# Forgetting attention: the causal mask moves from a matrix product into the own block's key terms

## The chip, the cores and the metric

One core of one Trainium2 chip. The metric is the device time of one launch in microseconds, the median of the runs shown.

## What is computed

The kernel computes two transformer blocks on 1024 tokens of width 1024 in float32. The first has 16 meta tokens in front, a Mamba-2 branch and a softmax attention with forget gates; the second has a differential and a dilated attention. The change touches the forgetting attention alone: 16 heads of 64, 1040 positions, taken in blocks of 128 queries.

```python
c = jnp.cumsum(logf, axis=1)
...
s = jnp.einsum("bthd,bshd->bhts", qi, k).astype(jnp.float32) * scale
s = s + (cqi[..., :, None] - c_k[..., None, :])
s = jnp.where(kpos[None, :] <= qpos[:, None], s, -jnp.inf)
p = jax.nn.softmax(s, axis=-1).astype(v.dtype)
return jnp.einsum("bhts,bshd->bthd", p, v)
```

The query's own term `cqi` is the same for all keys of a row and falls out of the softmax; the key term `-c_k` stays.

## The kernel before, in words

The heads are taken in eight pairs `p`, two heads `j` at a time. Each pair goes through the projections of its keys, queries and values (`fox_project`), the gate (`fox_gate`) and the attention (`fox_attend`). Generators yield after each step, and `merge` weaves the attention of a pair with the gate projection of the same pair (two halves, each 24 products of 512 columns, lines 112 to 114), then with the projections of the next pair. The engines run in the order in which this weaving writes the instructions; nothing is rescheduled later.

In `fox_attend` the key terms of a head are loaded into `cb`, the same row on all 128 partitions. A pair has eight query tiles `i`, each in three steps. `A(i)` makes the negated logits of 16 + 128(i+1) keys: for each head the keys are cut into one to three chunks of at most 512 columns, each in a PSUM bank of its own; two products (lines 566 and 567, the high and low parts of the operands) fill it, and for the last chunk a third product of a bf16 identity with a bf16 table adds 1e30 to the 128 columns of the query's own block where the key comes after the query (line 569). VectorE then adds the key terms to the bank, writes the sum to `N` and takes the running minimum of the row (line 570). Each reduction is followed by an instruction that reads the accumulator into one column of `mn`, and the reduction of the next chunk takes that column as its scalar. ScalarE computes the exponentials with the last column as bias (line 573), and GpSimd copies the 16 meta columns (line 576). `B(i)` transposes the blocks of `N` on TensorE (line 624) and evacuates them on ScalarE into `pt` (line 630). `C(i)` multiplies with the values for every fourth tile (lines 604 and 607), and VectorE multiplies the result with the gate (line 609).

`pipeline` writes these steps as A(0), A(1), then for each i: A(i+2), C(i-1), B(i). For one pair the order on TensorE is: A(0), first half of the gate, A(1), A(2), B(0), A(3), second half of the gate, B(1), A(4), B(2), A(5), B(3), A(6), C(3), B(4), A(7), B(5), then the projections of the next pair. The gate's halves are evacuated by ScalarE (line 519), then by VectorE (line 520).

The PSUM pool has eight banks in this part (line 75), all of one tag; each call of `bank` takes the next of the eight in turn, and the first writer waits until the last reader of that bank's previous content is done.

```python
self.psum(8, 0)
...
b = self.ps.tile([128, 512], F32, tag="bank", name="bank", bufs=self.one)
```

GpSimd's queue holds the 16-column copies and the subtractions that split the weights into a high and a low part (line 121); SyncE issues the loads of the weights and of `cb`.

Of the kernel before, what the change touches and what calls it, by code (L numbers as in the profile page):

```python
# [9 lines left out]
F32 = mybir.dt.float32  # L10
F32R = mybir.dt.float32r
BF16 = mybir.dt.bfloat16
I32 = mybir.dt.int32
AF = mybir.ActivationFunctionType
ALU = mybir.AluOpType
# [10 lines left out]
HUGE = 3e38  # L26
# [40 lines left out]
class Kern:  # L67
# [128 lines left out]
    def consts(self):  # L196
        nc, V, cst = self.nc, self.nc.vector, self.cst
        self.w32 = cst.tile([128, 32], F32, name="w32")
        V.memset(self.w32, 0.0)
        V.memset(self.w32[0:64, 0:1], 1.0)  # L200
        V.memset(self.w32[64:128, 1:2], 1.0)
        V.memset(self.w32[:, 2:3], 1.0)
        self.identb = cst.tile([128, 128], BF16, name="identb")
        self.maskb = cst.tile([128, 128], BF16, name="maskb")
        V.tensor_copy(out=self.identb, in_=self.ident)
        V.tensor_copy(out=self.maskb, in_=self.cm[:, 3, :])
        self.ones = cst.tile([128, 128], F32, name="ones")
        V.memset(self.ones, 1.0)
        a, b = PARAM_COLS["conv_w"]
        self.cwh = cst.tile([128, 120], F32, name="cwh")  # L210
        V.tensor_scalar(out=self.cwh, in0=self.params[:, a:a + 120], scalar1=0.5, scalar2=None, op0=ALU.mult)
        self.gbh = cst.tile([128, 16], F32, name="gbh")
        V.tensor_scalar(out=self.gbh, in0=self.pslot("gate_bias"), scalar1=0.5, scalar2=None, op0=ALU.mult)
        self.sb48 = cst.tile([48, 1], F32, name="sb48")
        V.tensor_tensor(out=self.sb48, in0=self.pslot("b48")[:48], in1=self.pslot("sgn")[:48], op=ALU.mult)
# [322 lines left out]
    def fox_attend(self, p, st):  # L538
        nc, te = self.nc, self.nc.tensor
        cb = []  # L540
        for j in range(2):
            c = self.ph.tile([128, L], F32, tag="cb", name="cb", bufs=2)
            nc.sync.dma_start(out=c, in_=self.d_csp[2 * p + j].partition_broadcast(128))
            cb.append(c)
        vT = st.pop("vT")
        st["vm"] = self.v_meta(vT)
        st["v"] = self.v_tokens(vT, [16 + 128 * b for b in range(8)])
        y = self.slot("y", w=T)
        Ns, PTs, M = {}, {}, [None, None]

        def A(i):
            if i % 4 == 0:
                M[i // 4] = self.ph.tile([128, 2, 128], F32, tag="bt", name="pm", bufs=2)
            W = 16 + 128 * (i + 1)
            n = -(-W // 512)
            w = -(-W // (2 * n)) * 2
            Ns[i] = []
            for j in range(2):
                N = self.slot("N")
                mn = self.sm.tile([128, 3], F32, tag="mn", name="mn", bufs=4)  # L560
                qt = st["q"][j][:, i * 128:(i + 1) * 128]
                for c in range(n):
                    s0, s1 = c * w, min(W, c * w + w)
                    S = self.bank()[:, :s1 - s0]
                    last = c == n - 1
                    te.matmul(S, qt, st["k"][j][0][:, s0:s1], start=True, stop=False)
                    te.matmul(S, qt, st["k"][j][1][:, s0:s1], start=False, stop=not last)
                    if last:
                        te.matmul(S[:, s1 - s0 - 128:], self.identb, self.maskb, start=False, stop=True)
                    nc.vector.tensor_tensor_reduce(  # L570
                        out=N[:, s0:s1], in0=cb[j][:, s0:s1], in1=S, scale=1.0,
                        scalar=mn[:, c - 1:c] if c else HUGE, op0=ALU.add, op1=ALU.min, accum_out=mn[:, c:c + 1])
                nc.scalar.activation(out=N[:, :W], in_=N[:, :W], func=AF.Exp, scale=-1.0, bias=mn[:, n - 1:n],  # L573
                                     accum_out=self.lall[:, 2 * p + j, i:i + 1])
                c = 32 * (i % 4) + 16 * j
                nc.gpsimd.tensor_copy(out=M[i // 4][:, 0, c:c + 16], in_=N[:, 0:16])
                Ns[i].append(N)
            return 4 * max(W, 512) / 2.4

        def B(i):  # L580
            if i % 4 == 3:
                ps = self.bank()
                te.transpose(ps[:, :128], M[i // 4][:, 0], self.ident)
                nc.vector.tensor_copy(out=M[i // 4][:, 1], in_=ps[:, :128])
            if i % 4 == 0:

                PTs[i // 4] = [[self.ph.tile([128, 4, 512], F32, tag="pt", name="pt", bufs=4) for _ in range(2)]
                               for _ in range(i // 4 + 1)]
            q = slice((i % 4) * 128, (i % 4 + 1) * 128)
            for j in range(2):  # L590
                self.transposes(Ns[i][j], 16, i + 1, [pt[j][:, :, q] for pt in PTs[i // 4]], act=True)
            del Ns[i]
            return 2 * (i + 1) * 109

        def C(i):
            if i % 4 != 3:
                return 0
            g = i // 4
            pt = PTs.pop(g)
            O = self.bank()  # L600
            for b in range(i + 1):
                c0 = max(0, b - 4 * g) * 128
                for j in range(2):
                    te.matmul(O[64 * j:64 * j + 64, c0:], st["v"][:, b, 64 * j:64 * j + 64],
                              pt[b // 4][j][:, b % 4, c0:], start=b == 0, stop=False)
            for t in range(4):
                te.matmul(O[:, t * 128:(t + 1) * 128], st["vm"][:, t], M[g][:, 1], start=False, stop=t == 3)
            c = slice((i - 3) * 128, (i + 1) * 128)
            nc.vector.scalar_tensor_tensor(out=y[:, c], in0=O, scalar=0.5, in1=st["zs"][:, c], op0=ALU.mult,
                                           op1=ALU.mult)  # L610
            return (2.5 + 4 * g) * 910

        yield from self.pipeline(8, A, B, C)
        nc.sync.dma_start(out=self.d_yatt[p], in_=y)

# [1198 lines left out]
```

## Time and profile before

| | us |
|---|---|
| median of 3 runs (2728.5 to 2733.69) | 2733.47 |
| the profiled execution | 2729.51 |
| its span | 2727.7 |

| engine | busy us | share of the span |
|---|---|---|
| TensorE, products | 2659.8 | 98% |
| VectorE | 1372.3 | 50% |
| ScalarE | 1165.6 | 43% |
| GpSimd | 684.5 | 25% |

PE is TensorE, PEld its weight loads, DVE VectorE, ACT ScalarE, POOL GpSimd. Products are pipelined: the next one starts before the one ahead has ended, and a product's end is modelled, so the time that it costs is read from the starts that follow each other. The forgetting attention lies between some 75 and 655 us of the span, in eight pairs of about 77 us. The granted clock of TensorE is full (0.994 over the execution).

### The profile page before, as it was taken

The numbers are of one execution on the slowest core, as the hardware profiler recorded it, in microseconds if no ns is written. First come the engines' busy times: TensorE is split into PE (matmuls) and PEld (weight loads), VectorE is DVE, ScalarE is ACT, GpSimd is POOL, SyncE is SP. The second block draws the span as 40 slices with busy tenths as digits, with TensorE's granted clock in tenths as the row PEclk, the third lists the DMA queues.
The fourth block names the chain that finished last, engine by engine and source line by source line (L and its number), as shares of the span: only waits on it lengthen the run. The fifth ranks groups of instructions, "written<-read, shape, count | busy, mean of one in ns | idle before, by whom it ended". The sixth has DMA issues, their size and how long they took to land. (4 is left out here: it accounts for less than half of the span.)

```text
span 2727.7 us, 38674 instructions
## 1 busy us (share of the span) xinstructions
PE 2659.8 (98%) x14925; PEld 2232.2 (82%) x14925; DVE 1372.3 (50%) x2761; ACT 1165.6 (43%) x2080; POOL 684.5 (25%) x764
## 2 busy tenths in 40 slices
PE   8999999999999999999999999999999999998999
PEld 6888888888989889889877887878877877777877
DVE  5433322233574573654756777444654555446332
ACT  5554444445343433443432123445644555445331
POOL 1112121111243342342432333111111121204321
PEclk9999999999999999999999999999999999998999
DMA  3122222221123123122168653340222223324422
GB/s 131 58 64 72 78 79 71 78 64 62 39 88 114 55 78 116 55 103 91 55 207 279 205 182 131 128 121 30 72 70 70 79 94 94 86 72 146 160 65 70
DMA packets 85464, 266.87 MB, mean 98 GB/s; under 512 B 10880, under 2 KB 12032, under 8 KB 84256
## 3 DMA queue, kind: packets, MB, share of 16 engines
q1 hardware_dynamic: 85280, 264.40, 30.3%
q8 instruction: 117, 1.92, 0.3%
q14 instruction: 67, 0.55, 0.1%
HBM read 205.57 MB, written 33.49 MB: 88 GB/s over the span
## 5 line engine op out<-in xcount | busy, mean ns | idle before, releaser
L121 POOL TENSOR_TENSOR wlo<-wraw,whi 128x1024 fp32r<-128x1024 f32 (+2 forms) x168 | 374.4, 2232 | 1288.7 <-ACT whi L120 1077.8
L112 PE MATMUL bank<-uh,whi 128*128 128x512 f32 (+4 forms) x1752 | 625.8, 357 | 0.1
L114 PE MATMUL bank<-uh,wlo 128*128 128x512 f32 (+4 forms) x1752 | 618.8, 353 | 0.1
L113 PE MATMUL bank<-ul,whi 128*128 128x512 f32 (+4 forms) x1752 | 618.5, 353 | 0.0
L114 PEld LDWEIGHTS bank<-uh,wlo 128*128 128x128 f32 (+1 forms) x1752 | 327.9, 187 | 35.4 <-POOL wlo L121 0.5
L112 PEld LDWEIGHTS bank<-uh,whi 128*128 128x128 f32 (+1 forms) x1752 | 328.3, 187 | 34.3 <-issue 1.1
L113 PEld LDWEIGHTS bank<-ul,whi 128*128 128x128 f32 (+1 forms) x1752 | 328.2, 187 | 32.3
L112 PE MATMUL bank<-u,whi 128*128 128x512 f32 x512 | 207.8, 406 | 0.7 <-ACT pr L935 0.7
L113 PE MATMUL bank<-u,whi 128*128 128x512 f32 x512 | 203.6, 398 | 0.0
L114 PE MATMUL bank<-u,wlo 128*128 128x512 f32 x512 | 203.3, 397 | 0.0
L120 ACT ACTIVATE whi<-wraw 128x1024 fp32r<-128x1024 f32 (+2 forms) x169 | 155.3, 926 | 20.5 <-DMA wraw<-in_w_pa_dram 18.2
L630 ACT ACTIVATE pt<-bank 128x512 f32<-128x512 f32 (+1 forms) x320 | 143.0, 509 | 44.8 <-PE bank L624 38.1
L114 PE MATMUL bank<-yh,wlo 128*128 128x512 f32 x384 | 152.5, 397 | 1.0 <-POOL wlo L121 0.8
L112 PE MATMUL bank<-yh,whi 128*128 128x512 f32 x384 | 152.3, 397 | 0.9 <-ACT whi L120 0.9
L113 PE MATMUL bank<-yl,whi 128*128 128x512 f32 x384 | 151.9, 395 | 0.0
L647 DVE SCALAR_TENSOR_TENSOR acc<-raw,cwh,acc 128x1040 f32<-128x1040 f32 x72 | 93.7, 1302 | 109.5 <-ACT acc L644 107.8
L573 ACT ACTIVATE N<-N,mn 128x272 f32<-128x272 f32 (+7 forms) x128 | 100.3, 786 | 45.2 <-DVE mn L570 44.0
L114 PEld LDWEIGHTS bank<-u,wlo 128*128 128x128 f32 x512 | 97.2, 190 | 23.2
L112 PEld LDWEIGHTS bank<-u,whi 128*128 128x128 f32 x512 | 97.8, 191 | 22.3 <-ACT pr L935 1.1
L113 PEld LDWEIGHTS bank<-u,whi 128*128 128x128 f32 x512 | 97.6, 191 | 20.7
L121 POOL TENSOR_TENSOR wo<-wl,wo 128x512 fp32r<-128x512 f32 x52 | 73.4, 1425 | 157.8 <-ACT wo L120 150.6
L624 PE MATMUL bank<-cm,N 128*128 128x128 f32 x832 | 106.9, 273 | 0.0
(326 smaller groups left out, 4961.5 us busy)
## 6 DMA issues: line engine op xcount, KB each, us to landing
wraw<-in_w_in_dram SPq DMA_DIRECT2D x120, 512.0 KB, 4.1
gt<-d_gate SPq DMA_DIRECT2D x48, 512.0 KB, 5.7
ab<-d_acs SPq DMA_DIRECT2D x32, 512.0 KB, 3.5
qs<-qt SPq DMA_DIRECT2D x48, 256.0 KB, 2.9
wl<-in_w_out_dram SPq DMA_DIRECT2D x48, 256.0 KB, 5.4
tab<-in_tab_dram SPq DMA_DIRECT2D x8, 1056.0 KB, 5.9
cb<-d_csp SPq DMA_DIRECT2D x16, 520.0 KB, 7.6
d_gate<-gt SPq DMA_DIRECT2D x16, 512.0 KB, 2.9
```

Source lines behind the costliest of these rows:

```text
L112: te.matmul(ps, lh, rh, start=start, stop=False)
L113: te.matmul(ps, lh, rl, start=False, stop=False)
L114: te.matmul(ps, ll, rh, start=False, stop=stop)
L120: self.nc.scalar.activation(out=hi, in_=src, func=AF.Copy)
L121: (self.nc.vector if vector else self.nc.gpsimd).tensor_tensor(out=lo, in0=src, in1=hi.bitcast(F32), op=ALU.subtract)
L573: nc.scalar.activation(out=N[:, :W], in_=N[:, :W], func=AF.Exp, scale=-1.0, bias=mn[:, n - 1:n], accum_out=self.lall[:, 2 * p + j, i:i + 1])
L624: nc.tensor.transpose(ps[:, b * 128:(b + 1) * 128], N[:, c:c + 128], self.ident)
L630: self.nc.scalar.activation(out=out, in_=ps, func=AF.Copy)
L647: V.scalar_tensor_tensor(out=acc[:, :L], in0=raw[:, k:k + L], scalar=w(k), in1=acc[:, :L], op0=ALU.mult, op1=ALU.add)
```

## The change

The identity and the mask in bf16 and the third product go away. For each query tile and head GpSimd adds the mask table to the 128 key terms of the own block, into a tile `cd` (`own_terms`). `A(i)` writes the sums of tile i+1 ahead of its own work, and `A(0)` those of tiles 0 and 1. VectorE's reduction of the last chunk is cut in two, the keys ahead of the own block with `cb` as before and the own block's 128 keys with `cd`; the running minimum goes through both, so `mn` has a fourth column.

```diff
-        self.identb = cst.tile([128, 128], BF16, name="identb")
-        self.maskb = cst.tile([128, 128], BF16, name="maskb")
-        V.tensor_copy(out=self.identb, in_=self.ident)
-        V.tensor_copy(out=self.maskb, in_=self.cm[:, 3, :])
...
+        CD = {}
+
+        def own_terms(i):
+
+            CD[i] = [self.sm.tile([128, 128], F32, tag="cd", name="cd", bufs=4) for _ in range(2)]
+            for c, k in zip(CD[i], cb):
+                nc.gpsimd.tensor_tensor(out=c, in0=k[:, 16 + 128 * i:144 + 128 * i], in1=self.cm[:, 3], op=ALU.add)
+
         def A(i):
...
+            if i == 0:
+                own_terms(0)
+            if i < 7:
+                own_terms(i + 1)
+            cds = CD.pop(i)
...
-                    last = c == n - 1
                     te.matmul(S, qt, st["k"][j][0][:, s0:s1], start=True, stop=False)
-                    te.matmul(S, qt, st["k"][j][1][:, s0:s1], start=False, stop=not last)
-                    if last:
-                        te.matmul(S[:, s1 - s0 - 128:], self.identb, self.maskb, start=False, stop=True)
-                    nc.vector.tensor_tensor_reduce(
-                        out=N[:, s0:s1], in0=cb[j][:, s0:s1], in1=S, scale=1.0,
-                        scalar=mn[:, c - 1:c] if c else HUGE, op0=ALU.add, op1=ALU.min, accum_out=mn[:, c:c + 1])
-                nc.scalar.activation(out=N[:, :W], in_=N[:, :W], func=AF.Exp, scale=-1.0, bias=mn[:, n - 1:n],
+                    te.matmul(S, qt, st["k"][j][1][:, s0:s1], start=False, stop=True)
+                    ends = [(s0, s1, cb[j][:, s0:s1])] if c < n - 1 else [(s0, s1 - 128, cb[j][:, s0:s1 - 128]),
+                                                                          (s1 - 128, s1, cds[j])]
+                    for a, b, k in ends:
+                        if a == b:
+                            continue
+                        nc.vector.tensor_tensor_reduce(
+                            out=N[:, a:b], in0=k, in1=S[:, a - s0:b - s0], scale=1.0,
+                            scalar=mn[:, m - 1:m] if m else HUGE, op0=ALU.add, op1=ALU.min, accum_out=mn[:, m:m + 1])
+                        m += 1
+                nc.scalar.activation(out=N[:, :W], in_=N[:, :W], func=AF.Exp, scale=-1.0, bias=mn[:, m - 1:m],
```

Three places of the instruction order show it, all from the first pair of heads; in brackets stand the queues that an instruction waits for. The first is VectorE at the first head of tiles 2 and 3 (line 582 is the reduction after the change; the short rows read the accumulator). Before:

```order
L570 ISA N_885,mn<-cb,bank 128x400 [waits DVE_49,PE_49]
L570 ISA mn 128x1
...
L570 ISA N_911,mn<-cb,bank 128x264 [waits PE_49,Activation_49]
L570 ISA mn 128x1
L570 ISA N_911,mn<-cb,bank,mn 128x264 [waits DVE_49,PE_49]
L570 ISA mn 128x1
```

Now:

```order
L582 ISA N_897,mn<-cb,bank 128x272 [waits PE_49]
L582 ISA mn 128x1
L582 ISA N_897,mn<-cd,bank,mn 128x128 [waits DVE_49,Pool_49]
L582 ISA mn 128x1
...
L582 ISA N_927,mn<-cb,bank 128x264 [waits PE_49,Activation_49]
L582 ISA mn 128x1
L582 ISA N_927,mn<-cb,bank,mn 128x136 [waits DVE_49,PE_49]
L582 ISA mn 128x1
L582 ISA N_927,mn<-cd,bank,mn 128x128 [waits DVE_49,Pool_49]
L582 ISA mn 128x1
```

Each head of each tile has one reduction and one read more, and the added piece waits for the read ahead of it and for GpSimd.

The second is TensorE after the change, from tile 3 to the second half of the gate projection (lines 575 and 576 were 566 and 567).

```order
L575 MATMUL bank<-kx_261,qs_559 128x264 [waits PE_49]
L576 MATMUL bank<-ky_262,qs_559 128x264
L575 MATMUL bank<-kx_261,qs_559 128x264 [waits DVE_49]
L576 MATMUL bank<-ky_262,qs_559 128x264
L575 MATMUL bank<-kx_263,qs_561 128x264 [waits DVE_49,PE_49]
L576 MATMUL bank<-ky_264,qs_561 128x264
L575 MATMUL bank<-kx_263,qs_561 128x264 [waits DVE_49,PE_49]
L576 MATMUL bank<-ky_264,qs_561 128x264
L112 MATMUL bank<-uh_1_88,whi_649 128x512 [waits DVE_49,PE_49]
```

The two masks that stood behind every last chunk are gone; the order is otherwise as before, and the projection's first product waits for VectorE.

The third is GpSimd. Before, the copies of tiles 0 to 2:

```order
L576 COPY pm<-N_811 128x16 [waits Activation_49,Pool_49]
L576 COPY pm<-N_820 128x16 [waits Activation_49]
L121 TENSOR_TENSOR wlo_831<-wraw_657,whi_830 128x1024 [waits DMAHW7_49,Activation_49]
L576 COPY pm<-N_867 128x16 [waits Activation_49]
L576 COPY pm<-N_876 128x16 [waits Activation_49]
L576 COPY pm<-N_885 128x16 [waits Activation_49]
```

Now:

```order
L553 TENSOR_TENSOR cd<-cb,cm 128x128 x2
L589 COPY pm<-N_815 128x16 [waits Activation_49]
L589 COPY pm<-N_824 128x16 [waits Activation_49]
L121 TENSOR_TENSOR wlo_835<-wraw_653,whi_834 128x1024 [waits DMAHW7_49,Activation_49]
L553 TENSOR_TENSOR cd<-cb,cm 128x128 [waits Pool_49]
L553 TENSOR_TENSOR cd<-cb,cm 128x128 [waits DVE_49]
L589 COPY pm<-N_875 128x16 [waits Activation_49]
L589 COPY pm<-N_884 128x16 [waits Activation_49]
L553 TENSOR_TENSOR cd<-cb,cm 128x128 [waits Pool_49]
L553 TENSOR_TENSOR cd<-cb,cm 128x128 [waits DVE_49]
L589 COPY pm<-N_897 128x16 [waits Activation_49]
```

The sums of tile i+1 stand between the copies of tile i-1 and those of tile i.

## Rows read from the trace of the kernel before

**Rows 1.** Page, part 1: busy us, share of the span, instructions of each engine.

```profile
PE 2659.8 (98%) x14925; PEld 2232.2 (82%) x14925; DVE 1372.3 (50%) x2761; ACT 1165.6 (43%) x2080; POOL 684.5 (25%) x764
```

**Rows 2.** Waits of PE, 70 to 655 us: us in total, times, longest.

```profile
PE bank L604 <- ACT pt L630: 5.6, 8, 0.8
PE bank L566 <- DVE mn L570: 1.4, 1, 1.4
```

**Rows 3.** Timeline of PE, first stretch: start us, us, line, tiles, [idle before].

```profile
317.57 0.28 PE L566 MATMUL bank<-kx,qs 128*128 128x264 f32 x1
317.69 0.28 PE L567 MATMUL bank<-ky,qs 128*128 128x264 f32 x1
317.81 0.23 PE L569 MATMUL bank<-maskb,identb 128*128 128x128 bf16 x1
317.85 0.37 PE L566 MATMUL bank<-kx,qs 128*128 128x264 f32 x1
318.06 0.28 PE L567 MATMUL bank<-ky,qs 128*128 128x264 f32 x1
...
318.42 0.23 PE L569 MATMUL bank<-maskb,identb 128*128 128x128 bf16 x1
318.46 0.48 PE L112 MATMUL bank<-uh,whi 128*128 128x512 f32 x1
318.78 0.39 PE L113 MATMUL bank<-ul,whi 128*128 128x512 f32 x1
319.01 0.39 PE L114 MATMUL bank<-uh,wlo 128*128 128x512 f32 x1
```

**Rows 4.** Timeline of DVE, first stretch (tile 1 from 316.91).

```profile
316.91 0.43 DVE L570 CUSTOM_DVE_ANT_0 N<-cb,bank 128x272 f32<-128x272 f32 x1
...
318.12 0.08 DVE L570 DVE_READ_ACCUMULATOR2_ANT mn<- 128x1 f32 x1
...
318.61 0.42 DVE L570 CUSTOM_DVE_ANT_0 N<-cb,bank 128x264 f32<-128x264 f32 x1
318.96 0.08 DVE L570 DVE_READ_ACCUMULATOR2_ANT mn<- 128x1 f32 x1
319.19 0.49 DVE L570 CUSTOM_DVE_ANT_0 N<-cb,bank,mn 128x264 f32<-128x264 f32 x1
319.60 0.08 DVE L570 DVE_READ_ACCUMULATOR2_ANT mn<- 128x1 f32 x1
```

**Rows 5.** Groups by form, DVE, 70 to 655 us: busy us, mean ns, idle before.

```profile
L570 DVE CUSTOM_DVE_ANT_0 N<-cb,bank,mn 128x456 f32<-128x456 f32 x16 | 11.0, 689 | 2.7 <-DVE mn L570 0.5
L570 DVE CUSTOM_DVE_ANT_0 N<-cb,bank,mn 128x264 f32<-128x264 f32 x16 | 7.8, 489 | 2.3
```

**Rows 6.** Timeline of DVE, second stretch and behind it.

```profile
324.92 0.69 DVE L520 SCALAR_TENSOR_TENSOR zs<-zs,bank 128x512 f32<-128x512 f32 x1 [4.25 <-ACT zs L519]
...
330.29 0.08 DVE L570 DVE_READ_ACCUMULATOR2_ANT mn<- 128x1 f32 x1
...
336.09 0.69 DVE L609 SCALAR_TENSOR_TENSOR y<-bank,zs 128x512 f32<-128x512 f32 x1 [2.73 <-PE bank L607]
```

**Rows 7.** Timeline of PE, second stretch.

```profile
323.86 0.40 PE L114 MATMUL bank<-uh,wlo 128*128 128x512 f32 x1
...
332.04 2.85 PE L604 MATMUL bank<-pt,vtok 128*64 128x512 f32 x16 [0.75 <-ACT pt L630]
```

**Rows 8.** Timeline of ACT, second stretch.

```profile
330.47 0.94 ACT L573 ACTIVATE N<-N,mn 128x784 f32<-128x784 f32 x1
...
331.40 1.07 ACT L630 ACTIVATE pt<-bank 128x512 f32<-128x512 f32 x2
```

**Rows 9.** Groups by form, POOL, whole span: busy us, mean ns, idle before.

```profile
L761 POOL TENSOR_TENSOR yq<-yq,th 128x128 f32<-128x128 f32 x128 | 60.7, 508 | 124.1 <-DVE yq L758 124.1
```

**Rows 10.** Timeline of POOL: the last copy of tile 3.

```profile
321.66 0.20 POOL L576 COPY pm<-N 128x16 f32<-128x16 f32 x1 [0.63 <-ACT N L573]
```

More of the change, by code (lines that the diff above doesn't have):

```diff
@@ L559, in A @@
                 N = self.slot("N")
-                mn = self.sm.tile([128, 3], F32, tag="mn", name="mn", bufs=4)
+                mn = self.sm.tile([128, 4], F32, tag="mn", name="mn", bufs=4)
                 qt = st["q"][j][:, i * 128:(i + 1) * 128]
+                m = 0
                 for c in range(n):
```

## The prediction

> **What bounds the kernel now.** I read the busy totals of the page first, then PE's waits in the attention part, then three timelines of one head pair, engine by engine. The totals [rows 1] say PE 98%, DVE 50%, POOL 25%: over the whole run TensorE is the limit. The waits of PE between 70 and 655 us [rows 2] say the same of this part: 5.6 us in eight waits for `pt`, 1.4 us in one wait for `mn`, nothing else. A reader who stops here concludes that 128 products fewer on PE are simply time won. The eight waits are the warning. There is one in each head pair, always at the product with the values (line 604), and it ends with ACT, not with PE. The eight pairs repeat a pattern of some 77 us, so I work one of them out, the one from 309 us on, and multiply.
>
> **What a mask product costs PE** [rows 3]. Inside a chunk of 264 keys the second product starts 0.12 us after the first (317.57, 317.69). The mask starts at 317.81, the next product at 317.85, and its follower at 318.06, 0.21 later instead of 0.12. So the mask takes 0.04 us itself and costs 0.09 more behind it: 0.13. Ahead of the gate projection it is the same: 0.04 (318.42 to 318.46), then 0.32 instead of 0.23 to the next start. Of a pair's 16 masks eleven stand ahead of such products; for the five ahead of a transposition or of line 604 I count half. That is 11 x 0.13 + 5 x 0.065 = 1.75 us of PE in a pair.
>
> **What the extra reduction costs DVE** [rows 4]. The 264-key reduction without `mn` holds the engine from 318.61 to its accumulator read at 318.96. The next one of the same row takes the running minimum as its scalar, so it starts only at 319.19, 0.23 after that read began. The 264-key form with `mn` then holds the engine 0.41 us (319.19 to 319.60). Means of 689 ns for 456 keys and 489 ns for 264 give 1.04 ns per key [rows 5], so 0.41 - 264 x 0.00104 = 0.135 us is its fixed part. Cutting 128 keys off a reduction leaves the number of elements as it was and adds one handover and one fixed part: 0.23 + 0.135 = 0.37 us, for each of two heads in each of eight query tiles. Bounds: 0.12 if only the fixed part were paid, 0.45 if the 0.21 us by which a duration exceeds its elements (489 - 275 ns) came on top of the handover. I take 0.37, since both parts stand in rows of the same reduction. In all DVE gets 128 x 0.37 = 47 us more.
>
> [...]
>
> **Where those 0.37 us fall.** Two stretches of a pair matter, both with DVE working without a pause.
>
> First stretch, query tiles 1 to 3, after the first half of the gate projection. DVE starts tile 1 at 316.91 [rows 4], when it has done the gate's product; that start hangs on the projection and doesn't move against it. PE runs ahead through tiles 1, 2, the transpositions of tile 0 and tile 3, then starts the gate's second half at 318.46 [rows 3]. There are eight PSUM banks, given out in turn (line 75, `bank`). Counting back from that projection: four banks of tile 3, two of the transpositions, tile 2's second head, and eighth, tile 2's first head. So line 112 must wait until that reduction is done; the order of the program has a wait for DVE at exactly this row. Before, the reduction's read starts at 318.12 and ends at 318.20, 0.26 us ahead of PE: just hidden. Now three extra pieces stand ahead of it: 318.20 + 3 x 0.37 = 319.31, and PE starts at about 319.36 instead of 318.46: **+0.9**, and the six masks of tiles 1 to 3 are won in vain.
>
> Second stretch, tiles 4 to 6. It again starts with DVE's gate product at 324.92 [rows 6], which waits for ACT and that for the projection's last product (323.86, [rows 7]), so it moves with PE. The softmax of tile 5, second head, starts on ACT at 330.47 [rows 8], 0.18 after DVE's last accumulator read of that tile began (330.29, [rows 6]): DVE sets it, to the hundredth. Next ACT evacuates `pt` of tile 3 (331.40), and PE, which has nothing else left, starts line 604 at 332.04 after 0.75 us of waiting [rows 7]. Now tiles 4 and 5 have four extra pieces ahead of that read: 4 x 0.37 = **+1.48** at line 604. The six masks of tiles 4 to 6 only make PE wait longer.
>
> Behind line 604 there is slack: DVE is idle 2.73 us ahead of 336.09 [rows 6], and all six pieces of tiles 4 to 6, 2.2 us, go into that. So only the masks of tiles 0 and 7 are gained, about 0.1 each between bounds of 0.04 and 0.13 (tile 0 has short products, tile 7 has a transposition behind one): **-0.4**.
>
> A pair: 0.9 + 1.48 - 0.4 = +1.98 us; eight pairs: **+15.8 us**. The profiled execution took 2729.51 us, some 4 us under the median of the runs shown, 2733.47; its sum would be 2745, and on the median it is 2749. The two casts that vanish from the start lie on DVE alone in the prologue, and I give them nothing.
>
> **GpSimd's part.** A sum of 128x128 takes 508 ns [rows 9]; two for a tile, 16 for a pair, 65 us in all on an engine busy for a quarter. In its queue the two sums for tile i+1 stand behind the two small copies of tile i-1, which wait for that tile's softmax. The sums for tile 4 can start after the copies of tile 2, about 320 us, and those for tile 5 after the copies of tile 3 (321.66, [rows 10]); DVE wants them from 326 and 329 on. Those for tiles 2 and 3 are nearer, yet have over a microsecond of room. Behind them in the queue stand copies and a weight split that PE wants much later. So they cost nothing; the cover would be gone if the sums came some 2 us later than worked out.
>
> **The rivals.**
>
> 1. PE stays the bound: DVE's extra work is hidden, as a busy share of 50% suggests, and the masks are won: 8 x 1.75 = 14 us, 2719. For it: PE's 98%. Against: the two places where PE already stands within 0.3 us of DVE or waits for what DVE set. Even pieces that cost nothing would let line 112 start at 318.25 instead of 318.46 and line 604 no earlier: -0.2 - 0.4 = -0.6 a pair, 5 us, 2728. So it decides only if the piece is nearly free. Chance 0.07.
>
> 2. The extra piece is cheap, since the handover overlaps or is shorter for 128 keys. [...] Against: the 0.23 us stand between every pair of chained reductions. Chance 0.13.
>
> 3. DVE waits for GpSimd too: a sum of tile i+1 is held up behind copies that wait for a softmax that DVE has made late, a loop over three engines. If in each stretch one tile waits a microsecond, the pair gets 2 us more: 16 us more, 2765. It decides when the sums are over 2 us later than now. For it: the copies do wait for ACT, again and again. Against: the room named above. Also here: a piece at 0.45 us or further banks that run out, up to 2758. Chance 0.09 for beyond 2758.
>
> That the sums are not made a tile ahead can be ruled out: the order shows them there.
>
> **How the numbers follow.** DVE paces both stretches, +6 to +24 us: 0.71. The likeliest time is 2749. At 0.25 us a piece a pair comes to +0.5 + 1.0 - 0.4 = 1.1, or 2742; at 0.45 to +1.14 + 1.8 - 0.4 = 2.5, or 2754. With rival 2 at the low end and some of rival 3 at the high end the range is 2736 to 2758. About 0.2%, 5.5 us, is what a measurement of this kernel tells from no change: faster 0.07, same 0.13, slower 0.80, which is the forecast and rival 3 together.
>
> **What would show it.** In the profile after, PE's waits in the attention part should grow from 7 us to over 20: line 604 for `pt` near 2.5 to 3 us each instead of 0.75, and a new wait for `mn` ahead of the gate projection and of tile 3's products, about 1.5 us a pair. The reductions should number 352 instead of 224, with 0.23 us between a read and the next piece. PE's busy time should fall while the span grows. Wrong would be: no wait for `mn`, line 604 as before, or DVE waiting for `cd`.

## The result, and the profile after

The changed kernel takes 2750.35 us (median of 5 runs, 2747.77 to 2753.11) against 2733.14 us (5 runs, 2728.5 to 2733.69) for the kernel before: ratio 1.0068, 95% interval 1.0056 to 1.0079, so 17.2 us slower. The forecast was 2749. The profiled execution took 2747.87 us, its span is 2746.1, 18.4 us above the span before.

Line numbers moved: 566 and 567 are now 575 and 576, 570 is 582, 573 is 586, 576 is 589, 604 is 617, 624 is 637, 630 is 643, 519 and 520 are 515 and 516. The busy totals of the page, which answer to [rows 1]:

```profile
PE 2653.3 (97%) x14797; PEld 2230.1 (81%) x14797; DVE 1400.4 (51%) x3015; ACT 1173.6 (43%) x2080; POOL 740.6 (27%) x892
```

TensorE does 128 instructions and 6.5 busy us less, and the kernel is longer. The waits of PE in the attention part, 70 to 680 us (us in total, times, longest), which answer to [rows 2], say where the time went:

```profile
PE bank L617 <- ACT pt L643: 12.3, 8, 1.6
PE bank L575 <- DVE mn L582: 5.4, 14, 1.9
PE bank L637 <- DVE mn L582: 5.0, 8, 1.0
PE bank L112 <- DVE mn L582: 2.9, 8, 0.4
PE bank L575 <- DVE zs L516: 1.6, 1, 1.6
PE bank L575 <- ACT pt L643: 1.5, 8, 0.2
```

They sum to 28.7 us where it was 7.0. Four of the six lines did not exist before, and three of the six name `mn`, the column that a reduction leaves behind: TensorE now waits for VectorE's reductions to give banks back.

One pair, the one that answers to [rows 3] and [rows 7]. Timeline of PE of the kernel after (start us, us, line, tiles, idle before):

```profile
326.78 0.36 PE L575 MATMUL bank<-kx,qs 128*128 128x264 f32 x1 [0.31 <-DVE mn L582]
...
327.50 0.36 PE L575 MATMUL bank<-kx,qs 128*128 128x264 f32 x1 [0.25 <-DVE mn L582]
...
328.36 0.47 PE L112 MATMUL bank<-uh,whi 128*128 128x512 f32 x1 [0.38 <-DVE mn L582]
...
333.77 0.39 PE L114 MATMUL bank<-uh,wlo 128*128 128x512 f32 x1
...
338.64 1.06 PE L637 MATMUL bank<-cm,N 128*128 128x128 f32 x8 [0.65 <-DVE mn L582]
...
343.36 2.86 PE L617 MATMUL bank<-pt,vtok 128*64 128x512 f32 x16 [1.55 <-ACT pt L643]
```

And of DVE in the same pair (it answers to [rows 4]):

```profile
325.83 0.30 DVE L582 CUSTOM_DVE_ANT_0 N<-cb,bank 128x144 f32<-128x144 f32 x1
...
327.27 0.43 DVE L582 CUSTOM_DVE_ANT_0 N<-cb,bank 128x272 f32<-128x272 f32 x1
327.63 0.09 DVE L582 DVE_READ_ACCUMULATOR2_ANT mn<- 128x1 f32 x1
327.86 0.35 DVE L582 CUSTOM_DVE_ANT_0 N<-cd,bank,mn 128x128 f32<-128x128 f32 x1
328.13 0.08 DVE L582 DVE_READ_ACCUMULATOR2_ANT mn<- 128x1 f32 x1
...
341.67 0.08 DVE L582 DVE_READ_ACCUMULATOR2_ANT mn<- 128x1 f32 x1
```

Tile 2's first head, 400 keys, takes 0.86 us from the start of its first reduction to its last read (327.27 to 328.13): 0.36 to the first read, 0.23 of handover (from the start of the read to the start of the reduction that takes its result), 0.27 for the own block. TensorE's line 112 starts 0.23 after that last read began, at 328.36: the eighth bank back. At the other end of the pair, tile 5's last read begins at 341.67, and ScalarE follows at 341.78 (the timeline of ACT, which answers to [rows 8]):

```profile
341.78 0.95 ACT L586 ACTIVATE N<-N,mn 128x784 f32<-128x784 f32 x1 [0.58 <-DVE mn L582]
```

Then come `pt` and, at 343.36, line 617. The chain DVE, ACT, PE of [rows 6 to 8] is all there, later by what VectorE got more to do.

How the loss adds up along the run is read from the start of line 604 (617) in the first, the second and the last pair. Timelines of PE, before:

```profile
101.32 2.85 PE L604 MATMUL bank<-pt,vtok 128*64 128x512 f32 x16 [0.36 <-ACT pt L630]
...
178.79 2.86 PE L604 MATMUL bank<-pt,vtok 128*64 128x512 f32 x16 [0.74 <-ACT pt L630]
...
638.61 2.86 PE L604 MATMUL bank<-pt,vtok 128*64 128x512 f32 x16 [0.75 <-ACT pt L630]
```

and after:

```profile
107.43 2.85 PE L617 MATMUL bank<-pt,vtok 128*64 128x512 f32 x16 [1.54 <-ACT pt L643]
...
186.12 2.86 PE L617 MATMUL bank<-pt,vtok 128*64 128x512 f32 x16 [1.58 <-ACT pt L643]
...
658.26 2.85 PE L617 MATMUL bank<-pt,vtok 128*64 128x512 f32 x16 [1.53 <-ACT pt L643]
```

The kernel after is 6.11 us late in the first pair, 7.33 in the second, 19.65 in the eighth: (19.65 - 7.33) / 6 = 2.05 us a pair from the second on, and 1.3 us come back behind the last. Below, "a pair" means this quotient, taken in the same way from each kernel's own trace against the trace before.

### The profile page after: what moved, and what is told of

Read it like the earlier page. It is cut to its first block, busy times and chain, and to the rows that moved or that the text cites. A ratio compares the mean times of both kernels' runs of the same rounds, so it can differ in the third digit from the quotient of the medians.

```text
span 2746.1 us, 38960 instructions
## 1 busy us (share of the span) xinstructions
PE 2653.3 (97%) x14797; PEld 2230.1 (81%) x14797; DVE 1400.4 (51%) x3015; ACT 1173.6 (43%) x2080; POOL 740.6 (27%) x892
```

## The experiments

Three theories. **Theory 1**, that of the prediction: VectorE's extra piece paces TensorE at two places, the bank that line 112 waits for (tiles 1 to 3) and the softmax of tile 5 ahead of line 604. **Theory 2**: each extra piece costs its share wherever it stands, by VectorE's total. **Theory 3**: GpSimd's sums cost, as work that VectorE waits for or by getting in its way. A thousandth in a ratio is 2.7 us.

### The cut alone, without GpSimd (e1)

The mask product is back, the sums are gone; only the last reduction is still cut in two.

```diff
+                    last = c == n - 1
+                    te.matmul(S, qt, st["k"][j][1][:, s0:s1], start=False, stop=not last)
+                    if last:
+                        te.matmul(S[:, s1 - s0 - 128:], self.identb, self.maskb, start=False, stop=True)
...
-                                                                          (s1 - 128, s1, cds[j])]
+                                                                          (s1 - 128, s1, cb[j][:, s1 - 128:s1])]
```

> The mask product is back and GpSimd adds nothing; VectorE's last reduction stays cut in two. Theory 1 (VectorE's extra piece paces TensorE, through the turn of the eight banks in tiles 1 to 3 and through the softmax of tile 5 ahead of line 604): +0.9 and +1.48 us a pair, 19 us, and some 2 us more in the first pair, where TensorE already waits for VectorE: 2752 to 2757, at least as slow as the change. Theory 2 (each piece costs its share wherever it stands; the change's 17 us are the loss by 128 pieces less 14 us won by 128 masks): 2733 + 31 = 2764. Theory 3 (GpSimd's sums are what costs): 2733, as before.

Measured: 2746.61 us, ratio 1.006 (1.0047 to 1.0073): 14.9 us over the 2731.67 of its runs of the kernel before, with no work of GpSimd added. That takes theory 3 away as the main cause, and theory 2's price is missed. Theory 1's own figure is missed too, from below, by 5 us or more. The timeline of DVE in this kernel, tile 2's first head in the same pair, says why:

```profile
325.59 0.43 DVE L584 CUSTOM_DVE_ANT_0 N<-cb,bank 128x272 f32<-128x272 f32 x1
325.95 0.08 DVE L584 DVE_READ_ACCUMULATOR2_ANT mn<- 128x1 f32 x1
326.07 0.35 DVE L584 CUSTOM_DVE_ANT_0 N<-cb,bank,mn 128x128 f32<-128x128 f32 x1
326.35 0.08 DVE L584 DVE_READ_ACCUMULATOR2_ANT mn<- 128x1 f32 x1
...
327.44 0.08 DVE L584 DVE_READ_ACCUMULATOR2_ANT mn<- 128x1 f32 x1
327.67 0.36 DVE L584 CUSTOM_DVE_ANT_0 N<-cb,bank,mn 128x136 f32<-128x136 f32 x1
```

From the read to the own block's piece it is 0.12 here (325.95 to 326.07), not 0.23; to the second chunk of tile 3 it is 0.23 still (327.44 to 327.67). In the changed kernel's instruction order the second chunk's reduction waits for two queues, DVE and PE, and the own block's piece for DVE and GpSimd (Pool). In this kernel the own block's piece reads nothing that GpSimd made. Its trace has 191 semaphore instructions at the line of the reduction, the changed kernel 318: 127 fewer, for 128 pieces. So a second queue to wait for seems to add to the handover. The whole cut costs 0.76 - 0.49 = 0.26 to 0.27 us here (before, 400 keys take 0.49: 318.12 to 318.61 in the timeline of [rows 4]). With 0.11 less for each of the seven pieces of the two stretches and about 0.4 more for the masks of tiles 0 and 7, theory 1 gives 2.05 - 0.77 + 0.4 = 1.68 us a pair; it was 1.71. This sum was made after the result.

### The mask product left out (e2)

```diff
-                    te.matmul(S, qt, st["k"][j][1][:, s0:s1], start=False, stop=not last)
-                    if last:
-                        te.matmul(S[:, s1 - s0 - 128:], self.identb, self.maskb, start=False, stop=True)
+                    te.matmul(S, qt, st["k"][j][1][:, s0:s1], start=False, stop=True)
```

Nothing takes the product's place: the own block is not causal in this kernel.

> The mask product is left out and nothing takes its place, so the own block is not causal; one reduction a chunk as before. Theory 1: TensorE gains the masks of tiles 0 and 7 and 0.2 us up to the bank's release in tile 3, 0.6 us a pair: 5 us, 2728, and line 604 waits longer than 0.75 us. Theories 2 and 3 (TensorE is the bound as long as VectorE does no more): 14 us, 2719.

Measured: 2728.52 us, ratio 0.9986 (0.9978 to 0.9995), 3.2 us less. This is the whole gain that the change could have here if its replacement were free, against 14 us of products by rows [rows 3]. TensorE, done sooner, waits longer at the same place (waits of PE in this kernel):

```profile
PE bank L602 <- ACT pt L628: 7.5, 8, 0.9
```

5.6 us became 7.5.

### Half of the tiles at a time (e3, e4)

Both kernels have the change in some tiles and the mask product in the others.

```diff
+            cut = (0, 3, 6, 7)
...
-            if i < 7:
+            if i + 1 in cut:
                 own_terms(i + 1)
...
+                    product = c == n - 1 and i not in cut
```

e4 is the same with `cut = (1, 2, 4, 5)`.

> The change in tiles 0, 3, 6 and 7 alone; tiles 1, 2, 4 and 5 keep the mask product and the uncut reduction. Half of the pieces and half of the masks. Theory 1: these pieces stand ahead of neither place, so they cost nothing, and the masks of tiles 0, 3 and 7 give about 0.6 us a pair: 2728. Theory 2: half of the change's loss, 2742. Theory 3: half of GpSimd's sums, 2742.

> The change in tiles 1, 2, 4 and 5 alone, the other half. Theory 1: the whole loss at both places, +0.9 + 1.48 us a pair, nothing won back: 2733 + 19 = 2752, with the first pair's extra up to 2755, slower than the whole change. Theories 2 and 3: half of the loss, 2742.

Measured: tiles 0, 3, 6 and 7 give 2727.29 us, ratio 0.9985 (0.9976 to 0.9993); tiles 1, 2, 4 and 5 give 2750.28, ratio 1.0066 (1.0053 to 1.008). The same number of pieces, 64, earns 4.4 us in one half and costs 18.6 in the other. Theory 2 would have them alike, so it falls. A pair gains 0.5 us in e3 and loses 2.35 in e4, 0.3 more than with the full change. Waits of PE in e4, where the three places show again:

```profile
PE bank L625 <- ACT pt L651: 8.1, 6, 1.4
PE bank L580 <- DVE mn L590: 4.9, 14, 1.8
PE bank L645 <- DVE mn L590: 4.7, 8, 0.7
```

In e3 a single wait for `mn` is left, 1.4 us, the one that the kernel before has too [rows 2].

### The own block without the running minimum (e5)

```diff
-                            scalar=mn[:, m - 1:m] if m else HUGE, op0=ALU.add, op1=ALU.min, accum_out=mn[:, m:m + 1])
+                            scalar=mn[:, m - 1:m] if m and k is not cds[j] else HUGE, op0=ALU.add, op1=ALU.min, accum_out=mn[:, m:m + 1])
```

The softmax is then shifted by the minimum over the own block alone instead of the row's. Any shift cancels in the quotient as long as no exponential overflows, which here rests on the data: the row's largest logit may not stand far above the own block's.

> The change, but the own block's reduction starts its minimum afresh instead of taking the running one, so the row's softmax is shifted by the own block's minimum alone. The piece no longer waits for the accumulator read ahead of it; the number of pieces, the products and GpSimd's sums are those of the change. The first run showed 0.12 us from a read to the next piece where the piece waits for one queue and 0.23 where it waits for two. Theory 1 with the handover as the price: the piece costs some 0.08 us instead of 0.37, so 0.0 in the first stretch, +0.3 in the second, -0.4 for tiles 0 and 7, about 0 a pair: 2729 to 2735. Rival (the number of pieces, or the wait for GpSimd's sum, is the price): near the change, 2745 to 2750.

Measured: 2731.8 us against 2732.12, ratio 1.0003 (0.9994 to 1.0012). All pieces, sums and the missing products are as in the changed kernel; only the dependence on the read is gone, and with it the loss. Timeline of DVE, the same head of tile 2:

```profile
320.34 0.43 DVE L582 CUSTOM_DVE_ANT_0 N<-cb,bank 128x272 f32<-128x272 f32 x1
320.70 0.08 DVE L582 DVE_READ_ACCUMULATOR2_ANT mn<- 128x1 f32 x1
320.70 0.28 DVE L582 CUSTOM_DVE_ANT_0 N<-cd,bank 128x128 f32<-128x128 f32 x1
320.91 0.08 DVE L582 DVE_READ_ACCUMULATOR2_ANT mn<- 128x1 f32 x1
```

The piece starts with the read, and the cut costs 0.57 - 0.49 = 0.08 us. Of the 0.37 us that it costs in the changed kernel, 0.29 are the handover and what hangs on it.

### GpSimd's sums alone (e6)

The kernel before, with the 128 sums made and read by nobody.

```diff
+        def own_terms(i):
+            for k in cb:
+                c = self.sm.tile([128, 128], F32, tag="cd", name="cd", bufs=4)
+                nc.gpsimd.tensor_tensor(out=c, in0=k[:, 16 + 128 * i:144 + 128 * i], in1=self.cm[:, 3], op=ALU.add)
```

> The kernel before, with GpSimd's 128 sums added and read by nobody. Theory 1: they are hidden on GpSimd, 2732 within 0.1%. Theory 3 (GpSimd's queue or its share of memory costs): slower, up to 2750.

Measured: 2731.51 against 2732.12, ratio 1.0001 (0.9992 to 1.001). The sums are free, as the prediction had them, except for 0.67 us in the first pair of this trace (last section); with e1 that ends theory 3 as the main cause. What e6 can't show is the price of waiting for a sum, since nobody reads these: by e1 it is 0.11 us for a piece, 0.77 a pair.

### The gate in quarters (e7, e8)

If a stretch of tiles without other work for TensorE between them is what lets VectorE set the pace, smaller pieces of the gate projection between the tiles should take the loss away. Two edits to either kernel:

```diff
-                                lambda ps, c0, c1: self.silu2(ps, zs[:, c0 - 16:c1 - 16]))
+                                lambda ps, c0, c1: self.silu2(ps, zs[:, c0 - 16:c1 - 16]), fine=True)
...
-            merge(att, zipped(self.fox_gate(p, st), ssd_dt), 1.5, stop=True)
+            merge(att, zipped(self.fox_gate(p, st), ssd_dt), 0.96, stop=True)
```

> The kernel before, with the gate projection handed out in four quarters instead of two halves: after tiles 0 and 2 and after the transpositions of tiles 2 and 3, so that TensorE has other work inside both stretches. Mask product and uncut reduction as before. Theory 1: the 0.75 us of waiting a pair go, some 6 us: 2727. Theory 2: nothing changes, since VectorE does the same work: 2732.

> The change with the same four quarters. Theory 1: the two stretches no longer run ahead of VectorE, so its pieces are hidden and the masks are won: up to 14 us faster than the kernel before with quarters, 2713 to 2722. Theory 2: the pieces cost as much as ever, 17 us slower than the kernel before with quarters, 2744 to 2750.

Measured: the kernel before gains, 2728.66 us, ratio 0.9985 (0.9976 to 0.9994); its eight waits at line 604 are gone. The changed kernel with quarters takes 2730.41, ratio 0.9992 (0.9983 to 1.0001). So the change costs 17.2 us with the gate in halves and 1.8 (2730.41 - 2728.66) with the gate in quarters, which theory 2 can't give. But e8 misses theory 1's figure by 8 us or more: it should have stood below e7 by the masks, and stands level with it or a little above. Waits of PE in e8 show what is left:

```profile
PE bank L575 <- DVE mn L582: 4.7, 10, 0.6
PE bank L637 <- DVE mn L582: 3.4, 7, 0.5
```

VectorE still gives banks back too late, only at more places and for less time at each.

### Quarters and no running minimum in the own block (e9)

Both edits, of e5 and of e8, together.

> The change with the gate in quarters and the own block's minimum started afresh; both parts ran apart before (2730 and 2732). With quarters alone TensorE still waits some 13 us for VectorE inside the two stretches. Theory 1: with pieces of 0.08 us those waits go and the masks' 14 us are won: 2714 to 2722, faster than the kernel before with quarters (2728.7). Rival (the quarters themselves cost TensorE what the masks give, or the masks were worth less): 2726 to 2731.

Measured: 2720.53 us against 2732.67, ratio 0.9956 (0.9943 to 0.997), as expected, and faster than both kernels. A pair gains 1.9 us. The largest group of waits for `mn` that is left, from PE's waits in this kernel:

```profile
PE bank L575 <- DVE mn L582: 1.7, 7, 0.2
```

Here the product's removal is worth what it is not worth in the order before: e9 stands 0.29% below e7, about 8 us of the 14 at which the rows price the products. Where the other 6 stay is not shown. The caution on the shift in e5 holds for this version too.

### The sums of the two heads in the other order (e10)

This asks whether the second queue waited for is what makes the handover 0.23 instead of 0.12. GpSimd makes the second head's sum first, so that a wait for the first head's covers both, and the second head's piece waits for DVE alone.

```diff
-            for c, k in zip(CD[i], cb):
+            for c, k in list(zip(CD[i], cb))[::-1]:
```

> The change with GpSimd's two sums of a tile in the other order, second head first. The first head's piece then waits for the later of the two sums, so the second head's piece waits for the accumulator read alone, one queue instead of two. If the second wait is what makes a handover 0.23 instead of 0.12 us, half of the pieces cost 0.26 instead of 0.37: one piece fewer at full price in the first stretch, two in the second, -0.33 us a pair, 2747 to 2748, and the rows show 0.12 for the second head alone. If something else sets the handover (the scalar, the size), 2750 and 0.23 for both.

Measured: 2745.23 us, ratio 1.0048 (1.0035 to 1.0061), 5 us under the changed kernel where 2 to 3 were expected. Timeline of DVE, tile 2's two heads:

```profile
325.23 0.08 DVE L582 DVE_READ_ACCUMULATOR2_ANT mn<- 128x1 f32 x1
325.46 0.35 DVE L582 CUSTOM_DVE_ANT_0 N<-cd,bank,mn 128x128 f32<-128x128 f32 x1
...
326.09 0.08 DVE L582 DVE_READ_ACCUMULATOR2_ANT mn<- 128x1 f32 x1
326.21 0.35 DVE L582 CUSTOM_DVE_ANT_0 N<-cd,bank,mn 128x128 f32<-128x128 f32 x1
```

0.23 for the head with two queues, 0.12 for the head with one, side by side in the same kernel with the same operands. The view of line 582 has what lies between them, the semaphore instructions in DVE's queue (count, ns least, median and most, first and last start). In the kernel after:

```profile
L582 DVEq EVENT_SEMAPHORE  x318: 21/21/50, 81.9 to 667.9; - x159
```

and here:

```profile
L582 DVEq EVENT_SEMAPHORE  x254: 21/21/50, 80.6 to 663.5; - x127
```

64 fewer, one for each second head of eight tiles in eight pairs: here a second queue to wait for is an instruction of its own. The new order also has a price: VectorE's reductions wait for GpSimd's sums seven times, 6.5 us in all, where the changed kernel has one wait for GpSimd of 0.5 us. A pair's time shows no sign of it. A pair costs 1.75 us instead of 2.05: 0.30 less, where three pieces of second heads (one in the first stretch, two in the second) times 0.11 make 0.33. Of the rest, 1.9 us lie in the first pair, whose line 617 starts at 105.57 instead of 107.43; 1.1 of these lie ahead of the attention and belong to no edit.

One other way out was not tried: a single uncut reduction whose key terms GpSimd would prepare for the whole last chunk. Whether on-chip memory has room for it is not shown.

## Why the prediction was right

**The forecast** was DVE pacing both stretches, 2749; it came to 2750.35. The steps in turn:

**The piece's price.** Worked out as 0.23 + 0.135 = 0.37 us; measured 0.86 - 0.49 = 0.37. The terms were right, and for the reason named, the handover between chained reductions, which e5 shows by taking it away (0.08 left). That the 0.23 carried over was in part luck: it was read at a reduction that waits for two queues, DVE and PE, and the new piece happens to wait for two as well, DVE and GpSimd; e1's piece, with one, has 0.12.

The lower bound of 0.12 was to be the fixed part alone, for which the rows give 0.135; the independent piece of e5 costs 0.08, less than that. e1's chained piece, 0.26 to 0.27, lies between the bounds. In e1, where the products stand as before, TensorE's waits from 70 to 680 us sum to 14.3 us instead of 7.0, and the run takes 15 us more.

**First stretch.** Predicted +0.9 at line 112. From the start of tile 1's first reduction to line 112 it is now 2.53 us (325.83 to 328.36), before 1.55 (316.91 to 318.46, [rows 3, 4]): +0.98. The sum let line 112 follow 0.13 us behind the start of the last read (0.08 to the read's end and 0.05 more); it follows by 0.23. So before the change TensorE had 0.11 us to spare there, not the 0.2 of rival 1.

**Second stretch.** Predicted +1.48 at line 604. From the gate's last product to line 617 it is 9.59 us (333.77 to 343.36), before 8.18 (323.86 to 332.04, [rows 7]): +1.41. One reading in it was too strong, that VectorE sets ScalarE's start at 330.47 to the hundredth [rows 6, 8]: ScalarE's row has no idle time ahead of it, so ScalarE came free at that moment too. Counted from the gate's last product, VectorE's read is 1.47 later (341.67 against 330.29) and ScalarE's start 1.40 (341.78 against 330.47); the 0.07 between them is the rest of the 1.48.

**The masks.** Predicted -0.4 a pair for tiles 0 and 7 and nothing for the rest: 0.98 + 1.41 - 2.05 = 0.34. e2 had 3.2 us for all eight pairs, which is 0.4 a pair; in its trace a pair gains 0.55 from the second on, of which 0.11 can be the room at line 112. e3 and e4 place the loss in the very tiles that the two stretches name.

**The pair**: +1.98 predicted, +2.05 measured. Eight pairs were to give 15.8 us.

**What was mis-sized.** Line 604's wait was to be 2.5 to 3 us each; it is 1.5 [rows 7 had 0.75]. Line 637 (0.65 in the pair shown) and line 575 take a share of the same delay ahead of it, since their banks come late by the same pieces; the start of line 617, which is what counts, is where it was predicted. The new waits ahead of tile 3 and line 112 sum to 0.94 in that pair (0.31, 0.25 and 0.38) instead of 1.5. GpSimd's sum takes 458 ns (median of 128) where 508 was taken from [rows 9], and the own block's piece waits for GpSimd once in 128 times, 0.5 us in the last pair.

**The first pair was not seen at all.** It is 6.11 us late instead of 2. In it VectorE comes to tile 0 late, from the Mamba branch's steps (lines 332 to 341 before), so TensorE and ScalarE wait for it from tile 0 on, which the pattern of the pair at 309 us doesn't have. Its parts: 1.06 us lie ahead of the attention (line 332 starts at 72.42 before, its counterpart 328 at 73.48 after; in e10, which makes the same sums, the like steps stand where they stood before, so I hold this for a difference between runs); 0.66 are VectorE's slower steps of the last section (72.42 to 80.70 before, 73.48 to 82.42 after); 0.74 are tile 0's two pieces. These three make 2.46, of which 2.29 arrive at the evacuation of the gate's first half on VectorE (83.40 before, 85.69 after). Line 112 is 3.45 late (86.96, 90.41), 1.16 more, which tiles 1 and 2 bring; then the clock adds 1.20 (last section). What is left of the 6.11, 1.46, is the second stretch, as in the other pairs (1.41). Between the first and the second pair 0.8 us less is added than in the others, and 1.3 us come back after the last; neither was followed up. These partly cancel, and that the total came so near the forecast owes something to this: 4.1 us more in the first pair, 0.8 and 1.3 less elsewhere, 2.0 us over the forecast; with 0.07 more in each other pair that is the 18.4 of the profiled executions, where 15.8 was forecast.

**The rivals.** Rival 1 (14 us won) is refuted by e2: leaving the mask out at no price gives 3.2 us in this order of the work, 6 at the most by its interval. Rival 2 was wrong for the changed kernel, and right for a piece without the running minimum (e5: no change). The low end of the range, 2736, rests on a price of the piece that no run shows; the runs have 0.08 (e5), 0.26 to 0.27 (e1) and 0.37 us (the changed kernel). Rival 3 did not happen, but for 0.5 us once.

## What to carry to other kernels

Cutting a reduction in two was cheap here only where the second part didn't take the first part's result: chained through an accumulator read it cost 0.26 us where the second part waited for VectorE alone, 0.37 where it waited for another engine too, and independent 0.08. VectorE, 51% busy over the run, still set the pace inside a pair (13.3 us of TensorE's waits end with its reductions); look at what the saturated engine does right behind its busiest stretch, and count banks back from there. If a piece of work is taken off the saturated engine, first ask with a kernel that leaves it out how much there is to gain: here 3 us, not 14, until the order of the work was changed as well.

## What the hardware showed

**A second queue to wait for lengthened the handover of a chained reduction.** From a read's start to the start of the reduction that takes its result: 0.12 us when the piece waits for DVE alone (e1, and the second heads of e10), 0.23 when it waits for DVE and one more queue, though the other had been done before (in the changed kernel tile 2's sums end at 324.78, and the read starts at 327.63) and the added instruction itself lasts 21 ns (median of 318). That is so in the changed kernel, in the first heads of e10, in the second chunks of the kernels before and after (0.22 to 0.24 in 95 of 96 each), and in those of tile 3 in e1, e5, e6 and e10 (0.22 to 0.23). Without the chain no price shows: a wait for GpSimd alone on work long done (e5, read and piece both at 320.70), or for PE and ScalarE (tile 3's first reduction in the changed kernel, in the first pair read and reduction both at 91.04). e1's 0.12 and 0.23, where the second queue is PE, speak for the second wait and against GpSimd's part in it.

**Steps of VectorE on SBUF alone took longer beside GpSimd's sums.** Timeline of DVE in the first pair, before:

```profile
79.59 0.46 DVE L339 SCALAR_TENSOR_TENSOR dt<-dt,dt 128x288 f32<-128x288 f32 x1
79.97 0.32 DVE L340 TENSOR_SCALAR dtx<-dtx 128x288 f32<-128x288 f32 x1
```

after, with GpSimd's sums running from 80.58 on:

```profile
80.80 0.60 DVE L335 SCALAR_TENSOR_TENSOR dt<-dt,dt 128x288 f32<-128x288 f32 x1
81.32 0.58 DVE L336 TENSOR_SCALAR dtx<-dtx 128x288 f32<-128x288 f32 x1
```

and with the sums alone (e6):

```profile
81.66 0.58 DVE L340 TENSOR_SCALAR dtx<-dtx 128x288 f32<-128x288 f32 x1
```

In e1, without sums, they take 0.46 and 0.32 as before. The own block's reductions, which have one input in PSUM, don't show it: they take 346 to 351 ns in all 128 cases, also where a sum runs beside them (330.08, with sums from 330.05 on).

**The clock in the first pair.** TensorE stands still for 1.58 us ahead of 86.43 and for 1.89 ahead of 88.83, and behind that the granted clock is 0.69 from 90 to 95 us. The view by windows (us, busy of PE, PEld, DVE, ACT, POOL with counts, granted clock, DMA share, GB/s), after:

```profile
90.00:95.00 5.00, 4.78 (x16) 3.69 (x16) 3.12 (x18) 3.48 (x11) 2.68 (x10) 0.69 0.00 0
```

and before:

```profile
90.00:95.00 5.00, 5.00 (x29) 3.92 (x28) 1.17 (x3) 1.32 (x6) 0.20 (x1) 1.00 0.02 3
```

In the timeline of PE (after) the gate's products there start 0.43 us apart, where they start 0.23 apart in [rows 3]:

```profile
88.83 0.36 PE L575 MATMUL bank<-kx,qs 128*128 128x264 f32 x1 [1.89 <-DVE mn L582]
...
90.97 0.63 PE L113 MATMUL bank<-ul,whi 128*128 128x512 f32 x1
91.40 0.63 PE L114 MATMUL bank<-uh,wlo 128*128 128x512 f32 x1
```

Six of them cost 1.20 us (90.41 to 93.11 instead of 86.96 to 88.46 before). In stretches of 1 us the granted clock there is 0.50 from 90 to 93, 0.94 from 93 to 94 and 1.00 from 94 to 95. e1, e4 and e10 show it too (0.79, 0.66 and 0.84 between 90 and 95 us), and e5 by its products, which start 0.42 to 0.43 apart from 88.88 to 91.87; e6 doesn't (1.00). So these waits of TensorE seem to cost more than their length there, though the traces show only that the low clock follows them. It happens once in the attention part: in stretches of 5 us from 70 to 680 the granted clock is under 1.00 from 85 to 95 alone (0.97 and 0.69), and in the pair that answers to [rows 3] the products start 0.24 apart again (328.67 and 328.91).
